# Four load buffers and an earlier queue place for the modulation in the first FFN rows, one power for the first norm

## The chip, the core and the metric

The kernel runs on one core of one Trainium2 chip. The metric is the device time of one execution in microseconds; lower is better. Three runs of the kernel before took 1579.51, 1582.39 and 1585.93 us, median 1582.39.

## The reference

One decoder block on x (256 tokens by 2048) with a condition vector c. Six modulation vectors of 2048 come from one large product with a single row, `mod = silu(c) @ w_ada + b_ada`, and w_ada is 2048 by 12288. The rest is matrix products with 256 rows:

```python
hn = rmsnorm(x, norm1_g) * (1 + sc1) + sh1
x = x + gt1 * hybrid_mixer(hn, ...)      # w_in, two causal mixers, dn_w_o, cf_w_o, w_out
hn = rmsnorm(x, norm2_g) * (1 + sc2) + sh2
gate, up = split(hn @ w_up)              # w_up 2048 x 11264
x = x + gt2 * ((silu(causal_dwconv(gate)) * up) @ w_down)
return rmsnorm(x, final_norm_g)
```

In the code the modulation pieces have the numbers j = 0 (sh1), 1 (sc1), 2 (gt1), 3 (sh2), 4 (sc2), 5 (gt2).

## The kernel before

**A product.** All large products go through `product` (L282). A weight comes in chunks of two rows of 128: a DMA of 512 KB into `w` (five buffers), ScalarE casts it to `wh` (L300, three buffers), VectorE takes the rest `wl = w - wh` (L302, three buffers), and TensorE does 12 matmuls of 512 columns with it (L289 to L291: two rows, two halves of the tokens, three terms). Two PSUM banks hold the result until `evac` takes it.

**The modulation runs beside the products.** `ada_block` (L131) makes one piece for one range of rows: for each of 16 rows of w_ada a load `ada_w` (L153, on SP's queue, 384 KB where the range is 768 wide), and a multiply-add of the loaded row on VectorE into `ada_acc` (L162). After the sixteenth row the sums over the partitions are taken: on TensorE six transposes of `ada_acc` (L86, tile `pt`), on VectorE a reduce of those (L191) and one addition that gives `mod` (L200). `ada_block` is a generator; `product` takes `side_rate` steps of it with each chunk (`credit`), and `need` (L211) takes all that is left of the named pieces at once.

**The FFN's first rows.** The 16 rows of w_up are cut into ranges, R3 = (0,4), (4,10), (10,16), so that products can start before all of hn2 is there. Of 22 products with w_up the first 12 (six groups, gate and up) run over range 0 (called part 0 here: 24 chunks, 288 matmuls), then all over range 1 (part 1: 36 chunks, 432 matmuls), then over range 2 together with what follows. Their sums stay in the tiles `part`. While part 0 runs, pieces 4 and 3 of the modulation are made for range 1, and while part 1 runs, for range 2. `modulate2(part)` (L889) then makes the range's tiles of hn2: `xn` (the norm's factor, L897 on ScalarE, L898 on VectorE), transposes (`turned`), and `split` (L257): `t` (L260, VectorE), hn's high part (L261, ScalarE), hn's low part (L262, VectorE). It needs `mod` of its range.

**What sets the order.** Each engine runs its own queue in order. The queues are made by a scheduler that plays the program through with bands of priority (`b_w`, `b_first`, `b_ada`), buffers and `issue_after` edges, so a change in one place can move instructions elsewhere too. A load waits on SP's queue until its buffer is free, and holds what stands behind it there.

**The first norm.** `rstd_col` (L223) gives the factor of one half of the tokens: a reduce on VectorE (L226), an addition (L227) and a power (L229) on GpSimd. L348 calls it for each half; then come eight scalings of `xt` (L352), transposes, and the sums of the first modulation pieces.

Later named in the text: the p1 stage (L396 on, 14 products over columns of w_in, each for two ranges, beside which pieces 1 and 0 of the modulation are made for the next range), and the cfo product (branch b's output, weights cf_w_o), which starts after a layer norm, whose silu pieces are `cfa` (L794) and whose input tiles are `cfh` (L828), beside the small matmuls of the DeltaNet (`bank`).

Of the kernel before, what the change touches and what calls it, by code (L numbers as in the profile page):

```python
# [55 lines left out]
def block_kernel(ctx: ExitStack, tc, x, vec, ab, rowv, w_ada, w_in, dn_w_o, cf_w_o, w_out, w_up, w_down, out):  # L56
# [28 lines left out]
    def turn(out, in_, n=P):  # L85
        nc.tensor.transpose(out=out, in_=in_, identity=ident[0:n, 0:n])  # L86
# [30 lines left out]
    A1, A2 = ([p0.tile([P, k1 - k0], F32, name=f"A{i}{k0}") for k0, k1 in R3] for i in (1, 2))  # L117
    av = w_ada.rearrange("(k p) n -> p k n", p=P)

    last_ada = [None]  # L120
    gt_rows, gt_home = {}, {}

    def gt_row(j, piece):
# [7 lines left out]
    def ada_block(j, part, pool, bufs, band=None, shared=False):  # L131
# [17 lines left out]
            pt = ps.tile([P, 512], F32, tag="tp", name="pt")  # L149
        for kc in range(0, KD, step):  # L150
            with band():
                wt = pool.tile([P, step, n], F32, tag="ada_w", bufs=bufs, name="ada_w")
                last_ada[0] = nc.sync.dma_start(out=wt, in_=av[:, kc:kc + step, c0:c0 + n]).ins  # L153
                for i in range(step):
                    k = kc + i
                    if shared and k % 3 == 2 and k < KD - 2:
                        for m in range(nk):
                            nc.tensor.matmul(pt[:, m:m + 1], lhsT=wt[:, i, m * P:(m + 1) * P], rhs=c_act[:, k:k + 1], start=(k == 2 and m == 0), stop=False, skip_group_check=True)
                    elif k == 0 and not as_row:
                        nc.vector.tensor_scalar(out=acc[:, 0:n], in0=wt[:, i, :], scalar1=c_act[:, k:k + 1], scalar2=None, op0=ALU.mult)  # L160
                    else:
                        nc.vector.scalar_tensor_tensor(out=acc[:, 0:n], in0=wt[:, i, :], scalar=c_act[:, k:k + 1], in1=acc[:, 0:n], op0=ALU.mult, op1=ALU.add)  # L162
            if kc + step < KD:
                yield
# [58 lines left out]
    def rstd_col(ms, t):  # L223

        a = p0.tile([P, 1], F32, tag="nrm_h", bufs=2, name="nrm_h")
        last_sum[0] = nc.vector.tensor_reduce(out=a, in_=ms[:, t, :], axis=mybir.AxisListType.X, op=ALU.add).ins  # L226
        nc.gpsimd.tensor_scalar(out=a, in0=a, scalar1=EPS, scalar2=None, op0=ALU.add)  # L227
        r = p0.tile([P, 1], F32, tag="nrm_c", bufs=2, name="nrm_c")
        nc.gpsimd.tensor_tensor(out=r, in0=a, in1=mhalf[:, 0:1], op=ALU.pow)  # L229
        return r  # L230
# [40 lines left out]
    def turned(src, tiles, pool=ps, tag="tp"):  # L271

        bank = pool.tile([P, 2, S], F32, tag=tag, name="turned")
        for i, j in enumerate(tiles):
            for t in range(2):
                turn(bank[:, i, t * P:(t + 1) * P], src[:, t, j * P:(j + 1) * P])
        return bank


# [43 lines left out]
    def rows(W, c0, k0=0):  # L323
        v = W.rearrange("(k p) n -> p k n", p=P)
        return lambda w, kc: [(w, v[:, k0 + kc:k0 + kc + 2, c0:c0 + 512])]
# [9 lines left out]
    with b_first():  # L335
        x_sb = p0.tile([P, KD, S], F32, tag="x", name="x_sb")
        xv = x.rearrange("(t p) n -> p t n", p=P)
        xt = p1.tile([P, 2, D], F32, tag="HS", name="xt")
        for q in range(2):
            for t in range(2):  # L340
                nc.sync.dma_start(out=xt[:, t, q * 1024:(q + 1) * 1024], in_=xv[:, t, q * 1024:(q + 1) * 1024])
        nc.sync.dma_start(out=vt, in_=vec)
        ss1 = p0.tile([P, 2, 2], F32, name="ss1")
        for q in range(2):
            for t in range(2):
                sq = p1.tile([P, 1024], F32, tag=("QA", "KA")[t], name="sq")
                nc.scalar.activation(out=sq, in_=xt[:, t, q * 1024:(q + 1) * 1024], func=AF.Square, scale=D ** -0.5, accum_out=ss1[:, t, q:q + 1])
        r1 = [rstd_col(ss1, t) for t in range(2)]  # L348
        for q in range(4):
            qs = slice(q * 512, (q + 1) * 512)  # L350
            for t in range(2):
                nc.vector.tensor_scalar(out=xt[:, t, qs], in0=xt[:, t, qs], scalar1=r1[t], scalar2=None, op0=ALU.mult)  # L352
            for i in range(2):
                k = 4 * q + 2 * i
                nc.scalar.copy(out=x_sb[:, k:k + 2, :], in_=turned(xt, (k, k + 1), pd, f"dl{i}"))
        for j in (1, 0):
            drain(ada_block(j, 0, sup, 6, shared=True))
        hn = p0.tile([P, 2, KD, S], F32R, tag="hn", name="hn")
        modulate(0)
# [529 lines left out]
    def modulate2(part):  # L889
        k0, k1 = R3[part]  # L890
        with b_first():
            xn = p2.tile([P, 2, (k1 - k0) * P], F32, tag="raw", name="xn")

            for a, b in ((k0, k0 + 2), (k0 + 2, k1)) if part == 0 else ((k0, k1),):
                at_ = slice((a - k0) * P, (b - k0) * P)
                with tc.issue_after(ada_after[0]) if part else nullcontext(), tc.issue_after(ada_after[1]) if part else nullcontext():
                    nc.scalar.activation(out=xn[:, 0, at_], in_=res[:, 0, a * P:b * P], func=AF.Copy, scale=r2[0])  # L897
                    nc.vector.tensor_scalar(out=xn[:, 1, at_], in0=res[:, 1, a * P:b * P], scalar1=r2[1], scalar2=None, op0=ALU.mult)  # L898
            for k in range(0, k1 - k0, 2):
                bank = turned(xn, (k, k + 1), pd, f"dl{k // 2 % 2}")  # L900
                for i in range(2):
                    c = slice(k + i, k + i + 1)
                    after = split(hn2, k0 + k + i, bank[:, i, :], A2[part][:, c], mod[3][part][:, c])
        return after
# [3 lines left out]
    ada_after[:] = modulate2(0)  # L908

    NG = 6  # L910
    pre = [p2.tile([P, 2, 512], F32, tag=f"h{g}{i}", name=f"part{g}{i}") for g in range(NG) for i in range(2)]
    for part in range(2):
        side_rate[0] = (1.2, 0.9)[part]
        for g in range(NG):
            for i, off in enumerate((0, FF)):
                product("up1", rows(w_up, off + 512 * g), R3[part], gh, gl, into(both(pre[2 * g + i]), part > 0))
        need((4, part + 1), (3, part + 1))
        modulate2(part + 1)
    for half, (g0, g1) in enumerate(((0, 6), (6, 11))):
        nt = 4 * (g1 - g0)  # L920
        hf = {}
# [38 lines left out]
            product("gate", rows(w_up, 512 * g), ks, gh, gl, evac_gate)  # L960
            product("up", rows(w_up, FF + 512 * g), ks, gh, gl, evac_up)
        if half == 0:
            raw = p2.tile([P, 2, D], F32, tag="raw", name="raw")
            for g in range(4):
                product("down", rows(w_down, 512 * g, 4 * g0), (0, nt), lambda k: hf[k // 4][0][:, k % 4, :], lambda k: hf[k // 4][1][:, k % 4, :], into(both(raw, g), False))
            continue
        need((5, 0), (5, 1))
        fg_row = p2.tile([P, D], F32, name="fg_row")
        nc.sync.dma_start(out=fg_row, in_=rowv[:, 2 * D:].to_broadcast([P, D]))
        with b_ada():  # L970
            for g in range(4):
                for d, r in zip(both(raw, g), both(res, g)):
                    nc.vector.tensor_tensor(out=d, in0=d, in1=gt_row(5, g), op=ALU.mult)
                    nc.vector.tensor_tensor(out=r, in0=d, in1=r, op=ALU.add)
        for g in range(4):
# [63 lines left out]
```

## Time and profile before

| | us |
|---|---|
| median of three runs | 1582.39 |
| profiled execution, device time | 1579.35 |
| profiled execution, span of the trace | 1577.6 |
| TensorE busy | 1522.2 (96%) |
| TensorE idle, the difference | 55.4 |
| VectorE busy | 1188.6 (75%) |
| ScalarE busy | 812.1 (51%) |
| GpSimd busy | 58.0 (4%) |

The profiled execution lies 3.0 us below the median. TensorE is busy all the time but for some 55 us, so the question for any change is which of those idle stretches it fills, and whether it opens new ones. The views that matter are the table of windows (busy time of each engine in a stretch, the granted clock PEclk, the busy share of the DMA engines and what they moved), and the timelines of the engines around an idle stretch, where a bracket says how long the engine stood idle before an instruction and which result ended the wait. Consecutive instructions overlap a little at their ends, so the step from one start to the next is shorter than the printed length.

### The profile page before, as it was taken

The page shows a single profiled execution, that of the slowest core. Times are in us where ns is not written, and L with a number is a line of the kernel's source. Part 1 is how long each engine was busy: PE and PEld are TensorE (multiplying, and loading weights), DVE is VectorE, ACT ScalarE, POOL GpSimd, SP SyncE. Part 2 cuts the span into 40 slices and gives each one's busy share as a digit, 9 for nine tenths or more (in the row PEclk, how much of TensorE's full clock was granted, in tenths as well). Part 3 has the DMA queues.
Part 4 walks back from the last instruction along what each step waited for, and adds up shares of the span by engine and source line. Part 5 has one row for each costly group of instructions (what it writes and reads, how often), then busy time and mean ns, then how long its engine had stood idle before and what let it go on. Part 6 is the DMA issues. An engine that isn't in the chain of part 4 may idle for free. (4 is left out here: it accounts for less than half of the span.)

```text
span 1577.6 us, 20092 instructions
## 1 busy us (share of the span) xinstructions
PE 1522.2 (96%) x7198; PEld 1257.7 (80%) x7198; DVE 1188.6 (75%) x1558; ACT 812.1 (51%) x1222; POOL 58.0 (4%) x120
## 2 busy tenths in 40 slices
PE   5999999999999999999989899999999999999997
PEld 5788887788888878788868687888888878888885
DVE  5889977689998978897577899887445677775554
ACT  3554444777687455544445334555434445454443
POOL 2000000400002000000000000000000000000000
PEclk9999999999999999999989999999999999999999
DMA  9999966534567738889779898655556777765552
GB/s 322 387 361 345 297 189 178 162 115 130 150 220 227 238 107 260 276 287 333 234 237 321 278 318 293 205 171 174 190 190 217 265 248 244 258 202 187 187 187 107
DMA packets 182284, 366.59 MB, mean 232 GB/s; under 512 B 12452, under 2 KB 30884, under 8 KB 182056
## 3 DMA queue, kind: packets, MB, share of 16 engines
q1 hardware_dynamic: 182184, 365.31, 69.6%
q8 instruction: 56, 0.92, 0.2%
q14 instruction: 44, 0.36, 0.1%
HBM read 363.17 MB, written 2.10 MB: 232 GB/s over the span
## 5 line engine op out<-in xcount | busy, mean ns | idle before, releaser
L300 ACT CAST wh<-w 128x1024 fp32r<-128x1024 f32 x488 | 512.8, 1052 | 579.4 <-PE mm_up L290 136.6
L302 DVE TENSOR_TENSOR wl<-w,wh 128x1024 fp32r<-128x1024 f32 x488 | 593.4, 1220 | 235.6 <-ACT wh L300 233.5
L162 DVE SCALAR_TENSOR_TENSOR ada_acc<-ada_w,c_act,ada_acc 128x768 f32<-128x768 f32 (+2 forms) x236 | 242.5, 1028 | 80.4 <-DMA ada_w<-in_w_ada 75.2
L290 PE MATMUL mm_up<-wh,hn 128*128 128x512 f32 x472 | 185.7, 394 | 2.9 <-DVE hn L262 2.9
L289 PE MATMUL mm_up<-wh,hn 128*128 128x512 f32 x472 | 184.8, 396 | 1.3 <-ACT wh L300 0.5
L291 PE MATMUL mm_up<-wl,hn 128*128 128x512 f32 x472 | 173.8, 396 | 1.5 <-DVE wl L302 1.4
L289 PE MATMUL mm_down<-wh,h 128*128 128x512 f32 x352 | 139.1, 395 | 0.0
L290 PE MATMUL mm_down<-wh,h 128*128 128x512 f32 x352 | 138.9, 395 | 0.0
L291 PE MATMUL mm_down<-wl,h 128*128 128x512 f32 x352 | 125.6, 395 | 0.0
L289 PE MATMUL mm_p<-wh,hn 128*128 128x512 f32 x280 | 109.4, 395 | 2.7 <-ACT hn L261 2.7
L290 PE MATMUL mm_p<-wh,hn 128*128 128x512 f32 x280 | 109.4, 392 | 0.0
L290 PEld LDWEIGHTS mm_up<-wh,hn 128*128 128x128 f32 x472 | 89.4, 190 | 21.6 <-DVE hn L262 3.4
L291 PEld LDWEIGHTS mm_up<-wl,hn 128*128 128x128 f32 x472 | 89.1, 189 | 21.7 <-DVE wl L302 3.5
L289 PEld LDWEIGHTS mm_up<-wh,hn 128*128 128x128 f32 x472 | 89.6, 190 | 20.4 <-issue 1.0
L291 PE MATMUL mm_p<-wl,hn 128*128 128x512 f32 x280 | 99.2, 392 | 0.0
L289 PE MATMUL mm_gate<-wh,hn 128*128 128x512 f32 x232 | 91.7, 395 | 0.0
L290 PE MATMUL mm_gate<-wh,hn 128*128 128x512 f32 x232 | 90.5, 390 | 0.0
L291 PE MATMUL mm_gate<-wl,hn 128*128 128x512 f32 x232 | 85.0, 392 | 0.2 <-DVE wl L302 0.2
L291 PEld LDWEIGHTS mm_down<-wl,h 128*128 128x128 f32 x352 | 66.3, 188 | 15.4
L290 PEld LDWEIGHTS mm_down<-wh,h 128*128 128x128 f32 x352 | 66.3, 188 | 15.4
L289 PEld LDWEIGHTS mm_down<-wh,h 128*128 128x128 f32 x352 | 66.3, 188 | 15.3
L441 DVE SCALAR_TENSOR_TENSOR cfa<-u,vt,cfa 128x256 f32<-128x256 f32 x176 | 75.8, 476 | 0.3
(308 smaller groups left out, 2483.3 us busy)
## 6 DMA issues: line engine op xcount, KB each, us to landing
w<-in_w_up SPq DMA_DIRECT2D x176, 512.0 KB, 4.4
w<-in_w_in SPq DMA_DIRECT2D x130, 512.0 KB, 4.2
ada_w<-in_w_ada SPq DMA_DIRECT2D x96, 512.0 KB, 4.9
ada_w<-in_w_ada SPq DMA_DIRECT2D x128, 384.0 KB, 5.3
w<-in_w_down SPq DMA_DIRECT2D x88, 512.0 KB, 3.6
w<-in_w_in SPq DMA_DIRECT2D x64, 256.0 KB, 3.9
w<-in_w_out SPq DMA_DIRECT2D x32, 512.0 KB, 5.5
w<-in_cf_w_o SPq DMA_DIRECT2D x16, 512.0 KB, 4.1
```

Of the source, the lines that this page charges most:

```text
L162: nc.vector.scalar_tensor_tensor(out=acc[:, 0:n], in0=wt[:, i, :], scalar=c_act[:, k:k + 1], in1=acc[:, 0:n], op0=ALU.mult, op1=ALU.add)
L289: nc.tensor.matmul(pts[t], lhsT=xh(k)[:, ts], rhs=wh, start=(k == k0), stop=False)
L290: nc.tensor.matmul(pts[t], lhsT=xl(k)[:, ts], rhs=wh, start=False, stop=False)
L291: nc.tensor.matmul(pts[t], lhsT=xh(k)[:, ts], rhs=wl, start=False, stop=(k == k1 - 1))
L300: nc.scalar.copy(out=wh, in_=w)
L302: nc.vector.tensor_tensor(out=wl, in0=w, in1=wh.bitcast(F32), op=ALU.subtract)
L441: nc.vector.scalar_tensor_tensor(out=acc[:, i, :], in0=us[g][:, i, k:k + S], scalar=V("cfconv", (2 * g + i) * CFK + k), in1=acc[:, i, :], ...
```

## The change

Three edits, of which two touch the FFN's first rows.

- **Load buffers.** In parts 0 and 1 every other load of `ada_w` goes to one of two further tiles (`raw2`, `raw3` in the pool `p2`), beside the two buffers it had. The tile `raw` of the later down product is cut into four tiles raw0 to raw3, and `xn` into two, raw0 and raw1.
- **Rate and place.** The rate of modulation steps is raised from 1.2 to 1.4 a chunk in part 0 and from 0.9 to 1.0 in part 1; `need` moves from behind the last product of a part to ahead of it; and the modulation steps that follow are ordered behind the newest range's row tiles (`ada_after` is set again for each part), where before they were ordered behind range 0's.
- **First norm.** One reduce, one addition and one power for both halves of the tokens.

```diff
@@ ada_block
-                wt = pool.tile([P, step, n], F32, tag="ada_w", bufs=bufs, name="ada_w")
+                if more[0] and kc // step % 2:
+                    wt = more[0].tile([P, step, n], F32, tag=f"raw{2 + kc // step // 2 % 2}", name="ada_w")
+                else:
+                    wt = pool.tile([P, step, n], F32, tag="ada_w", bufs=bufs, name="ada_w")
@@ first norm
-        r1 = [rstd_col(ss1, t) for t in range(2)]
+        a1 = p0.tile([P, 2], F32, name="a1")
+        nc.vector.tensor_reduce(out=a1, in_=ss1, axis=mybir.AxisListType.X, op=ALU.add)
+        nc.gpsimd.tensor_scalar(out=a1, in0=a1, scalar1=EPS, scalar2=None, op0=ALU.add)
+        nc.gpsimd.tensor_tensor(out=a1, in0=a1, in1=mhalf[:, 0:2], op=ALU.pow)
+        r1 = [a1[:, t:t + 1] for t in range(2)]
@@ modulate2
-            xn = p2.tile([P, 2, (k1 - k0) * P], F32, tag="raw", name="xn")
+            xn = [p2.tile([P, (k1 - k0) * P], F32, tag=f"raw{t}", name="xn") for t in range(2)]
@@ the FFN's first rows
+    more[0] = p2
     for part in range(2):
-        side_rate[0] = (1.2, 0.9)[part]
+        side_rate[0] = (1.4, 1.0)[part]
         for g in range(NG):
             for i, off in enumerate((0, FF)):
+                if (g, i) == (NG - 1, 1):
+                    need((4, part + 1), (3, part + 1))
+                    side_rate[0] = 0
                 product("up1", rows(w_up, off + 512 * g), R3[part], gh, gl, into(both(pre[2 * g + i]), part > 0))
-        need((4, part + 1), (3, part + 1))
-        modulate2(part + 1)
+        ada_after[:] = modulate2(part + 1)
@@ first down product
-            raw = p2.tile([P, 2, D], F32, tag="raw", name="raw")
+            more[0] = None
+            raw = [p2.tile([P, 2, 512], F32, tag=f"raw{g}", name="raw") for g in range(4)]
```

The scheduler's queues differ from before at several places. Line numbers of the changed kernel are three higher from L153 on, and seven to eleven higher behind L348.

**TensorE, part 0 of the FFN.** `pt<-ident,ada_acc` are the transposes with which the sums of piece 3 for range 1 begin. Before:

```order
L290 MATMUL mm_up_7634<-wh,hn_7041 128x512
L291 MATMUL mm_up_7634<-wl,hn_7041 128x512
L289 MATMUL mm_up_7635<-wh,hn_7041 128x512
L86 MATMUL pt<-ident,ada_acc 128x128 x6
L290 MATMUL mm_up_7635<-wh,hn_7041 128x512
L291 MATMUL mm_up_7635<-wl,hn_7041 128x512
L289 MATMUL mm_up_7634<-wh,hn_7041 128x512
```

These matmuls belong to the twelfth and last product of part 0; 274 of the part's 288 matmuls stand ahead of the transposes. Of the changed kernel:

```order
L293 MATMUL mm_up_7497<-wh,hn_7035 128x512
L294 MATMUL mm_up_7497<-wl,hn_7035 128x512
L292 MATMUL mm_up_7498<-wh,hn_7035 128x512
L86 MATMUL pt<-ident,ada_acc 128x128 x6
L293 MATMUL mm_up_7498<-wh,hn_7035 128x512
L294 MATMUL mm_up_7498<-wl,hn_7035 128x512
L292 MATMUL mm_up_7497<-wh,hn_7035 128x512
```

They now stand in the ninth product: 202 of the 288 matmuls are ahead of them. In part 1 the same transposes, for range 2, stood behind 634 of the 720 matmuls of both parts, and now stand behind 564; those of piece 4 move from 74 to 48, and from 436 to 384.

**SP, from the load of `fg_row` on, as part 0 begins.** Before:

```order
L969 DMA fg_row<-in_rowv 128x2048
L153 DMA ada_w<-in_w_ada 128x768 x3
L298 DMA w<-in_w_up 128x2x512
L153 DMA ada_w<-in_w_ada 128x768 x2
L298 DMA w<-in_w_up 128x2x512 x2
L153 DMA ada_w<-in_w_ada 128x768
L298 DMA w<-in_w_up 128x2x512 x3
L153 DMA ada_w<-in_w_ada 128x768 x2
L298 DMA w<-in_w_up 128x2x512
L153 DMA ada_w<-in_w_ada 128x768
L298 DMA w<-in_w_up 128x2x512
L153 DMA ada_w<-in_w_ada 128x768
```

Of the changed kernel:

```order
L980 DMA fg_row<-in_rowv 128x2048
L156 DMA ada_w<-in_w_ada 128x768 x6
L301 DMA w<-in_w_up 128x2x512
L156 DMA ada_w<-in_w_ada 128x768 x2
L301 DMA w<-in_w_up 128x2x512 x2
L156 DMA ada_w<-in_w_ada 128x768
L301 DMA w<-in_w_up 128x2x512
L156 DMA ada_w<-in_w_ada 128x768
L301 DMA w<-in_w_up 128x2x512
L156 DMA ada_w<-in_w_ada 128x768 x2
L301 DMA w<-in_w_up 128x2x512
L156 DMA ada_w<-in_w_ada 128x768
```

Eight loads of w_up stand ahead of this place in both. Behind it six modulation loads now stand in a row, where three stood. Counted on, of 18 loads left for the sums at the end of part 0 the last stands behind 11 further loads of w_up (18 before), and of 50 for those of part 1 the last stands behind 40 (48 before).

**ScalarE, from the activation table for silu to the last input of the cfo product's first rows.** Before:

```order
L613 COPY T_4128<-bank 64x256
L794 ACT_TABLE_LOAD
L794 ACTIVATE cfa_2983<-cfa_2983,vt 128x256 x2
L600 COPY P_3872<-bank 64x4x64
L794 ACTIVATE cfa_3133<-cfa_3133,vt 128x256 x2
L794 ACTIVATE cfa_3283<-cfa_3283,vt 128x256 x2
L828 CAST cfh<-cfa_2983 128x512
L600 COPY P_3920<-bank 64x4x64
L794 ACTIVATE cfa_3433<-cfa_3433,vt 128x256 x2
```

Of the changed kernel:

```order
L801 ACT_TABLE_LOAD
L801 ACTIVATE cfa_2977<-cfa_2977,vt 128x256 x2
L801 ACTIVATE cfa_3127<-cfa_3127,vt 128x256 x2
L835 CAST cfh<-cfa_2977 128x512
L801 ACTIVATE cfa_3277<-cfa_3277,vt 128x256 x2
L613 COPY U_3909<-bank 32x4x32 x2
L620 COPY T_4100<-bank 64x256
```

The first `cfh` now stands behind four silu pieces, where it stood behind six and a copy of `P`. On TensorE the first cfo matmuls now stand ahead of eight small matmuls of the DeltaNet that they stood behind.

## Rows read from the trace of the kernel before

**Rows 1.** The page, busy time of each engine and one of the costliest groups.

```profile
PE 1522.2 (96%) x7198; PEld 1257.7 (80%) x7198; DVE 1188.6 (75%) x1558; ACT 812.1 (51%) x1222; POOL 58.0 (4%) x120
...
L162 DVE SCALAR_TENSOR_TENSOR ada_acc<-ada_w,c_act,ada_acc 128x768 f32<-128x768 f32 (+2 forms) x236 | 242.5, 1028 | 80.4 <-DMA ada_w<-in_w_ada 75.2
```

**Rows 2.** Six windows of 20 us; columns are named in the first line.

```profile
core 0: us, PE busy (x) PEld busy (x) DVE busy (x) ACT busy (x) POOL busy (x), PEclk, DMA share, GB/s
580.00:600.00 20.00, 16.87 (x114) 12.83 (x113) 11.93 (x17) 14.35 (x34) 1.68 (x2) 0.83 0.29 84
840.00:860.00 20.00, 20.00 (x90) 16.57 (x89) 14.85 (x15) 11.95 (x16) 0.00 (x0) 1.00 0.94 327
860.00:880.00 20.00, 14.76 (x64) 11.37 (x63) 16.29 (x23) 8.95 (x14) 0.00 (x0) 0.91 0.89 302
880.00:900.00 20.00, 19.68 (x89) 15.98 (x88) 17.71 (x24) 7.52 (x9) 0.00 (x0) 1.00 0.80 256
940.00:960.00 20.00, 19.37 (x86) 15.20 (x85) 17.40 (x20) 7.38 (x7) 0.95 (x1) 1.00 0.91 308
960.00:980.00 20.00, 19.17 (x85) 15.19 (x84) 19.26 (x28) 8.41 (x12) 0.00 (x0) 1.00 0.84 282
```

**Rows 3.** Timeline of PE, 864 to 880 us: start, length, engine, line, operation, wait before.

```profile
864.21 0.81 PE L86 MATMUL pt<-ident,ada_acc 128*128 128x128 f32 x6
...
870.07 0.66 PE L86 MATMUL turned<-ident,xn 128*128 128x128 f32 x4 [1.81 <-DVE t L260]
...
874.11 0.80 PE L290 MATMUL mm_up<-wh,hn 128*128 128x512 f32 x1 [2.92 <-DVE hn L262]
...
877.62 0.40 PE L290 MATMUL mm_up<-wh,hn 128*128 128x512 f32 x1
...
879.19 0.50 PE L289 MATMUL mm_up<-wh,hn 128*128 128x512 f32 x1 [0.50 <-ACT wh L300]
```

**Rows 4.** Timeline of DVE, 801 to 874 us.

```profile
801.63 2.06 DVE L162 SCALAR_TENSOR_TENSOR ada_acc<-ada_w,c_act,ada_acc 128x768 f32<-128x768 f32 x2
...
862.22 1.02 DVE L162 SCALAR_TENSOR_TENSOR ada_acc<-ada_w,c_act,ada_acc 128x768 f32<-128x768 f32 x1 [0.66 <-DMA ada_w<-in_w_ada]
...
865.43 1.01 DVE L191 TENSOR_REDUCE ada_t<-pt 128x4 f32<-128x512 f32 x2
...
871.57 1.02 DVE L162 SCALAR_TENSOR_TENSOR ada_acc<-ada_w,c_act,ada_acc 128x768 f32<-128x768 f32 x1 [1.56 <-DMA ada_w<-in_w_ada]
872.50 1.22 DVE L302 TENSOR_TENSOR wl<-w,wh 128x1024 fp32r<-128x1024 f32 x1
873.64 0.75 DVE L262 TENSOR_TENSOR hn<-t,hn 128x256 fp32r<-128x256 f32 x2
```

**Rows 5.** Groups by line, DVE, 801.0 to 865.3 us: count, busy, mean ns, idle before.

```profile
L302 DVE TENSOR_TENSOR wl<-w,wh 128x1024 fp32r<-128x1024 f32 x22 | 26.6, 1218 | 0.4 <-ACT wh L300 0.4
L162 DVE SCALAR_TENSOR_TENSOR ada_acc<-ada_w,c_act,ada_acc 128x768 f32<-128x768 f32 x21 | 21.4, 1018 | 13.9 <-DMA ada_w<-in_w_ada 13.5
```

**Rows 6.** Timeline of PE, sums of the third range.

```profile
957.85 0.81 PE L86 MATMUL pt<-ident,ada_acc 128*128 128x128 f32 x6
```

**Rows 7.** Timeline of PE, first matmuls of the cfo product.

```profile
592.49 1.22 PE L289 MATMUL mm_cfo<-wh,cfh 128*128 128x512 f32 x2 [1.93 <-ACT cfh L828]
```

**Rows 8.** Timeline of POOL, first norm.

```profile
11.08 0.57 POOL L229 TENSOR_TENSOR nrm_c<-nrm_h,mhalf 128x1 f32<-128x1 f32 x1
...
13.51 0.74 POOL L229 TENSOR_TENSOR nrm_c<-nrm_h,mhalf 128x1 f32<-128x1 f32 x1
```

**Rows 9.** Timeline of DVE, third and fourth sums of the p1 stage.

```profile
150.45 1.01 DVE L162 SCALAR_TENSOR_TENSOR ada_acc<-ada_w,c_act,ada_acc 128x768 f32<-128x768 f32 x1
...
156.72 0.17 DVE L200 TENSOR_TENSOR mod<-pt,vt 128x6 f32<-128x6 f32 x1 [2.40 <-PE pt L180]
...
191.09 1.01 DVE L162 SCALAR_TENSOR_TENSOR ada_acc<-ada_w,c_act,ada_acc 128x768 f32<-128x768 f32 x1
...
198.82 0.15 DVE L200 TENSOR_TENSOR mod<-pt,vt 128x6 f32<-128x6 f32 x1
```

More of the change, by code (lines that the diff above doesn't have):

```diff
@@ L118, in block_kernel @@
     av = w_ada.rearrange("(k p) n -> p k n", p=P)
-    last_ada = [None]
+    last_ada, more = [None], [None]
     gt_rows, gt_home = {}, {}
@@ L275, in turned @@
             for t in range(2):
-                turn(bank[:, i, t * P:(t + 1) * P], src[:, t, j * P:(j + 1) * P])
+                turn(bank[:, i, t * P:(t + 1) * P], (src[t] if isinstance(src, list) else src[:, t, :])[:, j * P:(j + 1) * P])
         return bank
@@ L896, in modulate2 @@
                 with tc.issue_after(ada_after[0]) if part else nullcontext(), tc.issue_after(ada_after[1]) if part else nullcontext():
-                    nc.scalar.activation(out=xn[:, 0, at_], in_=res[:, 0, a * P:b * P], func=AF.Copy, scale=r2[0])
-                    nc.vector.tensor_scalar(out=xn[:, 1, at_], in0=res[:, 1, a * P:b * P], scalar1=r2[1], scalar2=None, op0=ALU.mult)
+                    nc.scalar.activation(out=xn[0][:, at_], in_=res[:, 0, a * P:b * P], func=AF.Copy, scale=r2[0])
+                    nc.vector.tensor_scalar(out=xn[1][:, at_], in0=res[:, 1, a * P:b * P], scalar1=r2[1], scalar2=None, op0=ALU.mult)
             for k in range(0, k1 - k0, 2):
@@ L962, in block_kernel @@
         if half == 0:
-            raw = p2.tile([P, 2, D], F32, tag="raw", name="raw")
+            more[0] = None
+            raw = [p2.tile([P, 2, 512], F32, tag=f"raw{g}", name="raw") for g in range(4)]
             for g in range(4):
-                product("down", rows(w_down, 512 * g, 4 * g0), (0, nt), lambda k: hf[k // 4][0][:, k % 4, :], lambda k: hf[k // 4][1][:, k % 4, :], into(both(raw, g), False))
+                product("down", rows(w_down, 512 * g, 4 * g0), (0, nt), lambda k: hf[k // 4][0][:, k % 4, :], lambda k: hf[k // 4][1][:, k % 4, :], into(both(raw[g]), False))
             continue
@@ L971, in block_kernel @@
             for g in range(4):
-                for d, r in zip(both(raw, g), both(res, g)):
+                for d, r in zip(both(raw[g]), both(res, g)):
                     nc.vector.tensor_tensor(out=d, in0=d, in1=gt_row(5, g), op=ALU.mult)
```

## The prediction

> **What bounds the kernel now.** I read the page's busy times first, then the windows over the span, then the timelines of the engines around each window in which TensorE is not busy for all of its time. The page shows a TensorE that works 1522.2 us of a span of 1577.6 [rows 1]: a change can win only in the 55 us of idle time, and in what the slower clock costs after them. The windows show where these lie: of those that the change can reach, 5.24 us at 860 to 880, 0.32 at 880 to 900, 0.63 and 0.83 at 940 to 980, and 3.13 at 580 to 600 (20 less PE's busy time [rows 2]). The start has some more.
>
> The stall at 864 to 880 is a chain. TensorE's transposes for the sums of piece 3 start at 864.21, with only 14 matmuls of the part behind them [rows 3]; VectorE reduces them at 865.43 [rows 4], and the row tiles of the next range need the result. TensorE waits 1.81 us for `t` and 2.92 us for hn's low part [rows 3]. The second wait is VectorE's queue: hn's low part starts at 873.64, behind a modulation step that itself sat 1.56 us waiting for its load, and behind a `wl` [rows 4]. The eight matmuls from 874.11 until 877.62 take 3.51 us [rows 3], where 90 in 20 us [rows 2] would take eight 1.78: the granted clock of the window is .91 [rows 2], and the matmuls behind the pause run at the lower of the two levels, 1.2 GHz in place of 2.4.
>
> Why the sums are so late: VectorE waits for loads of w_ada. From 801.0 to 865.3 it sits idle for 13.5 us for these loads, beside 21.4 us of steps and 26.6 us of `wl` [rows 5]; over the kernel the wait is 75.2 us [rows 1].
>
> **The change part by part.** All sums are against the profiled execution, 1579.35 us, which is 3.0 us under the median of the runs.
>
> *End of part 0.* The transposes of the sums move from behind 274 matmuls to behind 202, 72 x 0.222 = 16.0 us earlier, to about 848.2. The row tiles then have some 19 us (86 matmuls) before part 1's first product wants them; in the trace of before the way from the transposes to hn's low part took 873.64 - 864.21 = 9.4 us, with a load's wait in it. So the whole stall goes: idle 5.24 + 0.32, and 3.51 - 1.78 = 1.73 us of slow clock, 7.3 us. I leave 0.6 for the wait for a cast that stands in it too (0.50 at 879.19 [rows 3]): **-6.7**. What must hold for it is that the loads come sooner. Ahead of the sums stand, from VectorE's step at 801.63 on [rows 4], 18 loads of 0.393 MB and 11 of 0.524, 12.8 MB; until 848.2 less 1.5 us for the last steps that asks for 286 GB/s. The windows with two buffers moved 327 GB/s at a share of .94, 302 at .89, 256 at .80 and 308 at .91 [rows 2]; divided by the share, 320 to 348 GB/s with the DMA engines full, which four buffers bring nearer. VectorE's own work in that time, 21 steps of 1.02 and 14 `wl` of 1.22 by their means [rows 5], is 39 us of the 45.
>
> *End of part 1.* The same transposes stood at 957.85 [rows 6]; 70 matmuls earlier, less the 7.3 us won before, is 935. The idle 0.63 + 0.83 goes but for a little: **-1.3**. Here it is tight. 50 loads of w_ada and 40 of w_up, 40.6 MB, by 933.5 from 801.6 ask for 308 GB/s, and the lowest full rate above, 320, has them there at 928.5. VectorE's steps between the two sums (30 steps, 28 `wl`, 14 additions to `part`, the row tiles) come to 82 us by the printed means, and 77 by the steps from start to start, which are some 0.08 shorter (872.50 to 873.64 for a `wl` of 1.22 [rows 4]); there are 87. Between a stall of nothing and one of some 8 us, at 290 GB/s, I take nothing, since the rate that I ask for lies under all the full rates.
>
> *Layer norm and cfo.* A side effect of the scheduler. TensorE waited 1.93 us for `cfh` at 592.49 [rows 7], the window has 3.13 us of idle time and a clock of .83 [rows 2]. `cfh` now stands behind four silu pieces instead of six and a copy, and some small DeltaNet matmuls that ran before it now follow. At most the 3.13 us and a part of the clock go, some 4 us; at the least nothing, if the copies that moved behind are then waited for. I take the middle: **-2.0**.
>
> *First norm.* Of two powers, at 11.08 (0.57) and 13.51 (0.74) [rows 8], one stays, but it must wait for all four squares, so the first scalings come later and the last one at about the same time, half a us late. VectorE's first row tile stands ahead of one `wl` more, which is a step of 1.14 us [rows 4]. Between -1.1 and +0.7 I take **-0.4**, as the row tile is what the first product waits for.
>
> *p1 stage.* Here the queue moves the third and fourth sums 28 and 59 matmuls, 6.2 and 13.1 us, ahead. TensorE never waited there. After the last step (ends 151.46) `mod` came 5.3 us later, and after that of the fourth (ends 192.10) 6.7 us later [rows 9]; TensorE's sums take about 1.4 of these, so the slack was 3.9 and 5.3. If VectorE were no earlier, TensorE would now stall for 2.3 + 7.8 = 10 us; but ahead of the third sums its queue now holds two `wl` fewer, and ahead of the fourth seven and two additions, 2.3 and some 9 us of work: with the slack that covers 6.2 and 13.1, and the lower end is nothing. I take **+1.0**, near that end. The last sums, of piece 5, also move ahead, by 48 and 148 matmuls, where loads come singly; I put 0, and up to 2 in the range.
>
> The remaining waits (out product to FFN at 780 to 800, the end) keep their order: 0. **Sum:** -6.7 - 1.3 - 2.0 - 0.4 + 1.0 = -9.4, so 1570.0 on the profiled execution's scale, and with its 3.0 us to the median 1573.0, 0.6% faster. About 0.5%, 7.9 us, is what a measurement of this kernel can tell from no change.
>
> **The rivals.** *A, the loads hold TensorE at the earlier sums.* SP's queue is in order: a load of w_ada that waits for its buffer holds back the weights behind it, and the change puts more of them ahead of the weights. Up to the end of part 1 the lead of the weights over TensorE falls from 56 chunks issued at chunk 53 to 48 at chunk 47. For it: with two buffers some windows moved only 256 and 282 GB/s [rows 2], and VectorE was busy for 17.7 and 19.3 us of 20 in them. Against: the share was .80 and .84 in just these, so the DMA engines lacked loads, not speed. At 288 GB/s the 40.6 MB are there 9.4 us late, and all that is won is lost; at 270, within those rows, the stall is 18.4 us, with the slow clock behind it (1.7) the kernel takes 1579.35 - 9.4 + 20.1 = 1590.1, on the median's scale 1593. From 275 GB/s down it is slower by more than that 0.5%. The Trainium skill (DMA: Bandwidth & Descriptors, Anatomy of one DMA) says that DMA engines don't wait on semaphores: any wait happens on the issuing sequencer before dispatch. By that rule a blocked modulation load does hold the weights, and the trace of before agrees in so far as the share sank to .80 while VectorE waited for loads.
>
> *B, the p1 stage and the layer norm give it back.* The stall in the FFN goes, but TensorE waits at the earlier p1 sums, nearer the upper end (+6), and the layer norm's place wins nothing: 1579.35 - 6.7 - 1.3 - 0.4 + 6 = 1577, on the median's scale 1580, within 0.5%. For it: the slack of 3.9 and 5.3 us [rows 9] is less than the move. Against: VectorE's queue moved by the difference.
>
> *C, the change doesn't do what it says.* The two added buffers fill no sooner, since loads wait on SP behind weights that wait for theirs; the sums come when they came, and TensorE waits at them instead of at the row tiles. Of -8.0 at the two ends perhaps 3 is left: 1579.35 - 3 - 2 - 0.4 + 1 = 1575, on the median's scale 1578, within 0.5%.
>
> **How the numbers follow.** My forecast 0.60, A 0.14 (0.09 of it slower by over 0.5%), B 0.12, C 0.14. Of the forecast's own case 0.08 ends within 0.5%, by the spread of the layer norm and p1 terms; that gives faster 0.52, same 0.08 + 0.05 + 0.12 + 0.14 = 0.39, slower 0.09. Its own range is 1564 to 1579: the lower end takes -4 at the layer norm, -1.1 at the start, 0 in p1 and -7.3 at part 0's end, with the runs' 3 us under the median; the upper end takes 0 and +5 there. The range that holds 8 in 10 reaches on to B and C and to A's milder half: 1564 to 1585.
>
> **What would show it.** Right: no idle TensorE above 1 us between 840 and 980 and PEclk 1.00 there, the transposes of the sums at about 848 and 935 (some us earlier by what was won ahead), VectorE's wait for w_ada from 801 to 865 well under 13.5 us, and a DMA share near 1 at over 320 GB/s. The cfo product would start some 3 us earlier. Wrong: TensorE waiting for `ada_acc` at the transposes or for `wl` behind them (A); waits for `ada_acc` at the p1 sums (B); a wait for w_ada as long as before (C).

## The result and the profile after

Four runs of the changed kernel took 1562.68 to 1567.94 us, median 1564.44, against 1581.77 for four of the kernel before: ratio 0.9886, interval 0.9872 to 0.9900. It is 17.3 us faster, where 9.4 were forecast. A second set of six runs, later (e11 below), gave 1565.38 and ratio 0.9892 (0.9874 to 0.9910). The profiled execution took 1565.42 us, with a span of 1563.7.

The page after has less idle time of TensorE than the table before ([rows 1] and span: 55.4 us; now 51.4), but also 9.9 us less busy time for the same 7198 matmuls, which no part of the prediction had:

```profile
PE 1512.3 (97%) x7198; PEld 1252.9 (80%) x7198; DVE 1187.4 (76%) x1557; ACT 809.5 (52%) x1222; POOL 55.3 (4%) x118
...
L165 DVE SCALAR_TENSOR_TENSOR ada_acc<-ada_w,c_act,ada_acc 128x768 f32<-128x768 f32 (+2 forms) x236 | 242.3, 1027 | 51.3 <-DMA ada_w<-in_w_ada 49.8
```

The windows, with the columns of [rows 2] and one more stretch, 700 to 720:

```profile
core 0: us, PE busy (x) PEld busy (x) DVE busy (x) ACT busy (x) POOL busy (x), PEclk, DMA share, GB/s
580.00:600.00 20.00, 18.19 (x100) 12.78 (x98) 13.23 (x16) 14.35 (x29) 0.95 (x1) 0.91 0.44 129
700.00:720.00 20.00, 15.58 (x68) 11.94 (x67) 15.69 (x20) 6.28 (x7) 0.00 (x0) 1.00 0.96 352
840.00:860.00 20.00, 20.00 (x93) 16.62 (x92) 17.51 (x22) 11.21 (x15) 0.00 (x0) 1.00 0.99 358
860.00:880.00 20.00, 20.00 (x96) 16.54 (x95) 19.10 (x25) 12.51 (x18) 0.00 (x0) 1.00 0.91 317
880.00:900.00 20.00, 20.00 (x93) 16.62 (x92) 18.22 (x24) 7.38 (x7) 0.00 (x0) 1.00 0.96 342
940.00:960.00 20.00, 20.00 (x92) 16.55 (x91) 20.00 (x28) 9.98 (x14) 0.00 (x0) 1.00 0.77 248
960.00:980.00 20.00, 20.00 (x90) 16.57 (x89) 18.70 (x19) 7.72 (x8) 0.00 (x0) 1.00 0.84 283
```

In the FFN's first rows the forecast holds. From 840 to 980 TensorE is busy for all of the time and PEclk is 1.00, where 860 to 880 had 14.76 and .91. The DMA engines move 358 GB/s at a share of .99 in 840 to 860, where two buffers brought 327 at .94. The timeline of PE shows no wait at the sums and at the row tiles (compare [rows 3] and [rows 6]):

```profile
851.51 0.82 PE L86 MATMUL pt<-ident,ada_acc 128*128 128x128 f32 x6
...
861.26 0.60 PE L86 MATMUL turned<-ident,xn 128*128 128x128 f32 x4
...
873.09 0.38 PE L86 MATMUL turned<-ident,xn 128*128 128x128 f32 x2
...
876.08 0.81 PE L86 MATMUL turned<-ident,xn 128*128 128x128 f32 x6
...
936.37 0.82 PE L86 MATMUL pt<-ident,ada_acc 128*128 128x128 f32 x6
```

The transposes of the sums run at 851.51, those of the next range at 936.37, and the part's end is not waited for. The FFN now begins 4.0 us later (first mm_up at 802.49, before 798.51), so 851.51 is 49.0 us after its begin; the forecast 848.2 was 49.7. VectorE's wait for w_ada in the same window as [rows 5] falls from 13.5 to 1.6 us, with 26 steps in it where there were 21:

```profile
L165 DVE SCALAR_TENSOR_TENSOR ada_acc<-ada_w,c_act,ada_acc 128x768 f32<-128x768 f32 x26 | 26.3, 1013 | 1.9 <-DMA ada_w<-in_w_ada 1.6
L305 DVE TENSOR_TENSOR wl<-w,wh 128x1024 fp32r<-128x1024 f32 x20 | 24.4, 1222 | 3.1 <-ACT wh L303 3.0
```

The window 700 to 720 tells the other way: 15.58 us busy, where the kernel before had 19.92:

```profile
700.00:720.00 20.00, 19.92 (x94) 16.32 (x93) 17.07 (x22) 9.32 (x15) 0.00 (x0) 1.00 0.93 336
```

TensorE waits for weights in the out product: five waits with 5.98 us of idle time from its first matmul to its last, where the kernel before had one of 0.08. These are rows of PE, ScalarE and VectorE of the changed kernel there:

```profile
717.49 0.50 PE L292 MATMUL mm_out<-wh,mg 128*128 128x512 f32 x1 [2.28 <-ACT wh L303]
...
719.68 0.74 PE L294 MATMUL mm_out<-wl,mg 128*128 128x512 f32 x2 [0.98 <-DVE wl L305]
```

```profile
716.39 1.04 ACT L303 CAST wh<-w 128x1024 fp32r<-128x1024 f32 x1 [3.03 <-DMA w<-in_w_out]
```

```profile
717.74 0.75 DVE L165 SCALAR_TENSOR_TENSOR ada_acc<-ada_w,c_act,ada_acc 128x512 f32<-128x512 f32 x1 [3.01 <-DMA ada_w<-in_w_ada]
```

ScalarE waited 3.03 us for a load of w_out, VectorE 3.01 us for a load of w_ada, while the DMA engines were nearly full (share .96 in that window). The queue suggests why: loads of the modulation and of x stand ahead of the weight. On SP's queue of the changed kernel, two loads of w_ada and four of x (512 KB each) stand with one weight between them just ahead of that place; before, the modulation loads stood singly there, and a weight stood among the loads of x.

The place of the whole difference, by the first and last matmul of each product (column before to after, both profiled executions, us):

| stretch | before | after | difference |
|---|---|---|---|
| start to first mm_p | 42.98 | 40.91 | -2.07 |
| p1 stage (to first mm_qkv) | 198.52 | 200.05 | +1.53 |
| to last mm_ga | 331.87 | 329.11 | -2.76 |
| last mm_ga to first mm_cfo | 19.12 | 15.64 | -3.48 |
| first mm_cfo to first mm_out | 106.29 | 109.16 | +2.87 |
| first to last mm_out | 91.02 | 98.92 | +7.90 |
| to first mm_up | 8.71 | 8.70 | 0 |
| first mm_up to first mm_gate (FFN's first rows) | 179.42 | 168.59 | -10.83 |
| to first mm_down | 110.66 | 110.16 | -0.50 |
| first to last mm_down | 477.02 | 470.42 | -6.60 |

Two of the large differences, +7.9 and -6.6, lie where I had put 0. The third row, -2.76, has no cause in the change: kernels with the same queues there give 329.0 to 331.9 from one execution to the next.

### The profile page after: what moved, and what is told of

It is laid out like the page before. It is cut to its first block, busy times and chain, and to the rows that moved or that the text cites. A ratio compares the mean times of both kernels' runs of the same rounds, so it can differ in the third digit from the quotient of the medians.

```text
span 1563.7 us, 20087 instructions
## 1 busy us (share of the span) xinstructions
PE 1512.3 (97%) x7198; PEld 1252.9 (80%) x7198; DVE 1187.4 (76%) x1557; ACT 809.5 (52%) x1222; POOL 55.3 (4%) x118
## 5 line engine op out<-in xcount | busy, mean ns | idle before, releaser
L294 PE MATMUL mm_up<-wl,hn 128*128 128x512 f32 x472 | 170.5, 393 | 0.0
L292 PE MATMUL mm_down<-wh,h 128*128 128x512 f32 x352 | 137.2, 390 | 0.0
L293 PE MATMUL mm_down<-wh,h 128*128 128x512 f32 x352 | 136.9, 389 | 0.0
L293 PEld LDWEIGHTS mm_down<-wh,h 128*128 128x128 f32 x352 | 66.1, 188 | 13.7
L294 PEld LDWEIGHTS mm_down<-wl,h 128*128 128x128 f32 x352 | 66.1, 188 | 13.7
L292 PEld LDWEIGHTS mm_down<-wh,h 128*128 128x128 f32 x352 | 66.1, 188 | 13.5
```

What stands on the lines that cost most here:

```text
L292: nc.tensor.matmul(pts[t], lhsT=xh(k)[:, ts], rhs=wh, start=(k == k0), stop=False)
L293: nc.tensor.matmul(pts[t], lhsT=xl(k)[:, ts], rhs=wh, start=False, stop=False)
L294: nc.tensor.matmul(pts[t], lhsT=xh(k)[:, ts], rhs=wl, start=False, stop=(k == k1 - 1))
```

## The experiments

The experiments are numbered e1 to e12; each is named where it begins.

**The slower matmuls of the down product.** The mean step from the start of one matmul to the next, by the timeline and without the steps across waits and at the lower clock, was 0.2324 us in mm_down, 0.2324 in mm_cfo and 0.2329 in mm_dno before, and 0.2265, 0.2289 and 0.2276 after, at PEclk 1.00 in both; mm_up, mm_gate and mm_p had 0.227 to 0.228 in both. For mm_down the page's groups show the same as the mean length of one. Before:

```profile
L289 PE MATMUL mm_down<-wh,h 128*128 128x512 f32 x352 | 139.1, 395 | 0.0
L290 PE MATMUL mm_down<-wh,h 128*128 128x512 f32 x352 | 138.9, 395 | 0.0
```

After:

```profile
L292 PE MATMUL mm_down<-wh,h 128*128 128x512 f32 x352 | 137.2, 390 | 0.0
L293 PE MATMUL mm_down<-wh,h 128*128 128x512 f32 x352 | 136.9, 389 | 0.0
```

No instruction of these products differs. What differs is where tiles lie: in the built program every tile from p0's later part on lies elsewhere. The first theory, and its test (e1), an unused tile at the place of `a1`:

```diff
+        p0.tile([P, 2], F32, name="pad")
         r1 = [rstd_col(ss1, t) for t in range(2)]
```

> The kernel before with one unused tile of 8 bytes a partition in p0 at the place where the change puts a1: no instruction moves, but every later tile of SBUF lies 32 bytes higher. Theory 'offset' (matmuls whose stationary tiles lie behind p0 ran at a step of 0.2324 us before and 0.2265 after because those tiles moved by 32 bytes): step of mm_down 0.227, of mm_cfo and mm_dno too, 1056 x 0.0059 + 384 x 0.005 = about 8 us less than before, ratio 0.995. Rival 'other' (the split of raw, the queues' order, or the run set the step): step 0.232 and ratio 1.000.

Measured: ratio 1.0006 (0.9988 to 1.0023), steps 0.2330 in mm_down and 0.2330 in mm_dno.

```profile
L289 PE MATMUL mm_down<-wh,h 128*128 128x512 f32 x352 | 139.4, 396 | 0.0
L290 PE MATMUL mm_down<-wh,h 128*128 128x512 f32 x352 | 138.8, 394 | 0.0
```

The theory falls: moving every later tile by 32 bytes does nothing. The converse (e2), the changed kernel with such a tile behind `a1`:

```diff
         a1 = p0.tile([P, 2], F32, name="a1")
+        p0.tile([P, 2], F32, name="pad")
```

> The changed kernel with the same unused tile added, so that its tiles lie 32 bytes past a multiple of 64 again; no instruction moves. 'Offset': step of mm_down 0.232, about 8 us slower than the change, near 1572. 'Other': as the change, 1564.

Measured: 1565.17 us, ratio to before 0.9894 (0.9877 to 0.9910), step of mm_down 0.2271. The theory falls here too. But of the four kernels that ran together the two with the first norm's edit (e2 and e4, below) had the short step and the two without it (e1 and e3) the long one: the edit does set it, by something else than 32 bytes. In the built programs the tiles of the first norm have other places in p0 after the edit, which moves hn, w, wh and wl by 96 bytes down and the tiles of the pools behind p0 by 32 up. The address of a product's stationary tile less that of the first `wh`, modulo 256:

| stationary tile, product | before | after | e1 | e2 |
|---|---|---|---|---|
| hn, mg: mm_p, mm_up, mm_gate, mm_out | 0 | 0 | 0 | 0 |
| cfh, DeltaNet's output, h: mm_cfo, mm_dno, mm_down | 128 | 0 | 128 | 0 |

The address of h alone, modulo 256, can't be it: it is 64 both in the change (step 0.2265) and in e1 (0.2330).

The second theory, a distance, with a tile that moves the pools behind p0 alone (e5):

```diff
+    p0.tile([P, 32], F32, name="pad")
     r2, r3 = [], []
```

> The kernel before with an unused tile of 128 bytes a partition at the end of p0: hn, w, wh and wl stay, the tiles of the pools behind p0 (cfh, the DeltaNet's output, h) lie 128 bytes higher, and no instruction moves. Theory 'distance' (the step of a matmul is 0.232 us where its stationary tile lies 128 bytes past a multiple of 256 from wh, and 0.227 at a multiple of 256; before 128 for cfo, dno and down, 0 for all products over hn and mg; the change 0 for all): step of mm_down 0.2265, mm_dno 0.2275; 1056 x 0.0059 + 384 x 0.005 = 8 us less than before, ratio 0.995. Rival 'queue' (the order that the first norm's edit sets off makes the step): 0.232, ratio 1.000.

Measured: ratio 0.9964 (0.9948 to 0.9979), 6.3 us less by the medians; steps 0.2271 in mm_down, 0.2274 in mm_dno, 0.2287 in mm_cfo. The groups:

```profile
L289 PE MATMUL mm_down<-wh,h 128*128 128x512 f32 x352 | 137.2, 390 | 0.0
L290 PE MATMUL mm_down<-wh,h 128*128 128x512 f32 x352 | 137.0, 389 | 0.0
```

The same line in the changed kernel, at the same place (e6):

```diff
+    p0.tile([P, 32], F32, name="pad")
     r2, r3 = [], []
```

> The changed kernel with the same unused tile of 128 bytes at the end of p0, which puts the stationary tiles of cfo, dno and down 128 bytes past a multiple of 256 from wh. 'Distance': step of mm_down 0.232, 8 us slower than the change, near 1572 to 1573. 'Queue': 0.2265, 1564 to 1565.

Measured: 1572.77 us (1567.9 to 1575.18), 7 to 8 us over the change; step of mm_down 0.2330, of mm_dno 0.2325. The groups:

```profile
L292 PE MATMUL mm_down<-wh,h 128*128 128x512 f32 x352 | 139.7, 397 | 0.0
L293 PE MATMUL mm_down<-wh,h 128*128 128x512 f32 x352 | 138.6, 394 | 0.0
```

Adding and taking away agree, with no instruction moved: where these tiles lie relative to those of p0 sets the step. That it is the distance to `wh`, the tile that these matmuls read beside them, is the likeliest reading; `hn`, `w` and `wl` keep their places relative to `wh` in all these kernels. A third distance, 64 bytes more than before, so 192 (e10):

```diff
+    p0.tile([P, 16], F32, name="pad")
     r2, r3 = [], []
```

> The kernel before with an unused tile of 64 bytes a partition at the end of p0, no instruction moved: the stationary tiles of cfo, dno and down lie 192 bytes past a multiple of 256 from wh. If only a multiple of 256 is fast: step of mm_down 0.232, ratio 1.000. If only 128 is slow: 0.2265, ratio 0.996.

Measured: ratio 0.9976 (0.9963 to 0.9989), step of mm_down 0.2291. The groups:

```profile
L289 PE MATMUL mm_down<-wh,h 128*128 128x512 f32 x352 | 138.7, 394 | 0.0
L290 PE MATMUL mm_down<-wh,h 128*128 128x512 f32 x352 | 137.2, 390 | 0.0
```

Neither expectation: 192 lies between. Here only the group of L289 is long (394), the other is at 390.

**The parts of the change.** The FFN edits without the first norm's, with the tile of e1, so at distance 128 (e3); against the changed kernel:

```diff
-        a1 = p0.tile([P, 2], F32, name="a1")
...
-        r1 = [a1[:, t:t + 1] for t in range(2)]
+        p0.tile([P, 2], F32, name="pad")
+        r1 = [rstd_col(ss1, t) for t in range(2)]
```

> The FFN edits alone (buffers, rates, place of the sums) on the kernel before, with the unused tile, first norm as before. Up to the FFN its queues are those of before. Theory: 'offset' gives 8, the FFN's stretch 10.8 as in the change, and no TensorE waits for wl or wh in the out product appear, since those come from the order that the first norm's edit sets off: about 1563. Rival (the waits in the out product come with the FFN edits, whose loads move ahead): 1571, with waits of some 6 us for wl and wh at 700 to 760.

Measured: 1568.02 us, ratio 0.9914 (0.9896 to 0.9932); from the first mm_up to the first mm_gate 168.44 us; out product 91.1 us. The FFN's gain and the out product's loss are apart, as the theory had it; the 8 us of the first theory's placement are not there, so the time is higher by some 5 than the 1563 expected.

The first norm's edit alone (e4); against the kernel before:

```diff
-        r1 = [rstd_col(ss1, t) for t in range(2)]
+        a1 = p0.tile([P, 2], F32, name="a1")
+        nc.vector.tensor_reduce(out=a1, in_=ss1, axis=mybir.AxisListType.X, op=ALU.add)
...
+        r1 = [a1[:, t:t + 1] for t in range(2)]
```

> The first norm's edit alone; its new tile a1 also moves the later tiles by 32 bytes. Theory: start and layer norm win some 6, p1 loses 1.5 and the out product 8, as in the change, so the FFN begins 4 us later than before; the FFN's own stall stays; the down products win 6.2: about 2 us under before, ratio 0.9985. Rival (the out product's loss belongs to the FFN edits): 10 under before, ratio 0.994. If 'offset' is wrong: 4 us slower than before.

Measured: 1580.85 us, ratio 0.9997 (0.9983 to 1.0010). The out product takes 97.4 us, with these waits of TensorE from 690 to 770 (total, times, longest):

```profile
PE mm_out L291 <- DVE wl L302: 3.5, 4, 1.5
PE mm_out L289 <- ACT wh L300: 1.4, 1, 1.4
```

So the edit that was to save a power at the start wins 2 us there and some at the layer norm, gains 6 to 8 us by the distance, which it changes as a by-product, loses 2 in p1 and 6 to 7 in the out product by the order that it sets off, and ends where it began.

Only the FFN edits, at distance 0 (e7); against the changed kernel:

```diff
-        a1 = p0.tile([P, 2], F32, name="a1")
...
-        r1 = [a1[:, t:t + 1] for t in range(2)]
+        r1 = [rstd_col(ss1, t) for t in range(2)]
...
+    p0.tile([P, 32], F32, name="pad")
     r2, r3 = [], []
```

> The FFN edits alone, first norm as before, with the tile of 128 bytes at the end of p0. 'Distance': 8 us under the FFN edits with the other placement (1568.0), so 1560, and under the change, since the waits in the out product that the first norm's edit brings are not there. 'Queue': 1568.

Measured: 1562.04 us, ratio 0.9868 (0.9849 to 0.9886), 6.0 under e3 where 8 were expected. TensorE's only wait in the out product:

```profile
PE mm_out L292 <- ACT wh L303: 1.6, 1, 1.6
```

The buffers alone, with raw and xn cut as in the change (e8; the lines of that cut are left out here); against the kernel before:

```diff
+                if more[0] and kc // step % 2:
+                    wt = more[0].tile([P, step, n], F32, tag=f"raw{2 + kc // step // 2 % 2}", name="ada_w")
+                else:
...
+    more[0] = p2
...
+            more[0] = None
```

> The two further load buffers alone (raw and xn cut as in the change), with the rates, need and the order of before; first norm as before. In the queue the sums move as in the change in part 0 (behind 202 matmuls) and to 586 in part 1. Theory (the loads were what made the sums late, so the buffers carry the gain): from the first mm_up to the first mm_gate 169 to 171 us, as with all FFN edits (168.5; before 179.4); total about 1569 to 1571. Rival (the rates and the place of need carry it): 176 us or more, 1578 or more.

Measured: 1569.03 us, ratio 0.9904 (0.9880 to 0.9927); first mm_up to first mm_gate 169.20. Its windows, columns as above:

```profile
840.00:860.00 20.00, 20.00 (x95) 16.60 (x94) 17.59 (x23) 12.18 (x18) 0.00 (x0) 1.00 0.99 357
860.00:880.00 20.00, 20.00 (x94) 16.45 (x93) 18.93 (x24) 11.56 (x17) 0.00 (x0) 1.00 0.92 318
880.00:900.00 20.00, 20.00 (x93) 16.62 (x92) 18.23 (x24) 7.47 (x8) 0.00 (x0) 1.00 0.92 320
```

VectorE's wait for w_ada from 801.0 to 865.3:

```profile
L165 DVE SCALAR_TENSOR_TENSOR ada_acc<-ada_w,c_act,ada_acc 128x768 f32<-128x768 f32 x26 | 26.3, 1013 | 2.0 <-DMA ada_w<-in_w_ada 1.8
```

That is e3's time (1568.02) to within the noise, at the same distance: the buffers carry the gain. They do two things at once: the loads come sooner, and the scheduler puts the sums of part 0 behind 202 matmuls, where they stood behind 274. Which of the two would do alone was not tried. The rates and places alone (e9):

```diff
-        side_rate[0] = (1.2, 0.9)[part]
+        side_rate[0] = (1.4, 1.0)[part]
...
+                if (g, i) == (NG - 1, 1):
+                    need((4, part + 1), (3, part + 1))
+                    side_rate[0] = 0
...
-        need((4, part + 1), (3, part + 1))
-        modulate2(part + 1)
+        ada_after[:] = modulate2(part + 1)
```

> The raised rates, the earlier need and the order edges alone, with two load buffers and the first norm as before. In the queue the sums stay where they were (behind 274 matmuls in part 0, 649 in part 1). Theory (the loads are the limit): the stall at the end of part 0 stays, from the first mm_up to the first mm_gate 177 to 185 us, total as before, ratio 0.998 to 1.003. Rival (rates and place give part of the gain of 11): 174 us or less, ratio 0.996 or less.

Measured: ratio 0.9994 (0.9983 to 1.0005), stretch 180.94 us. The stall stays, with waits of 2.63 and 3.45 us, where the kernel before had 1.81 and 2.92:

```profile
861.98 0.82 PE L86 MATMUL pt<-ident,ada_acc 128*128 128x128 f32 x6
...
868.62 0.66 PE L86 MATMUL turned<-ident,xn 128*128 128x128 f32 x4 [2.63 <-DVE t L260]
...
873.18 0.80 PE L290 MATMUL mm_up<-wh,hn 128*128 128x512 f32 x1 [3.45 <-DVE hn L262]
```

VectorE's wait for w_ada in the same window stays too:

```profile
L162 DVE SCALAR_TENSOR_TENSOR ada_acc<-ada_w,c_act,ada_acc 128x768 f32<-128x768 f32 x20 | 20.4, 1018 | 15.4 <-DMA ada_w<-in_w_ada 15.1
```

Last, the change (e11) and the best version, that of e7 (e12), again, on one chip:

> The changed kernel again, beside the next kernel on one chip, to compare the two. As before: ratio 0.988 to 0.990.

> The FFN edits with the first norm as before and the tile of 128 bytes at the end of p0, again. If leaving the first norm's edit out wins what its order costs in the out product: some 2 to 3 us under the changed kernel on the same chip, ratio 0.986 to 0.988. If the lead of the earlier run came from the chip: the same as the change.

Measured: 1565.38 us (ratio 0.9892, 0.9874 to 0.9910) and 1563.38 (0.9874, 0.9853 to 0.9894). The best version lies 2.0 us under the change here and 2.4 in the earlier runs, which were on different chips; the intervals overlap, so that it is ahead is likely and not settled.

## Why the prediction was right or wrong

The direction was right and the size was wrong: 9.4 us were forecast, little more than half of the 17.3 measured, and the time lies only just inside the range. Two steps failed. The sum put at 0 whatever was not idle time of TensorE: the down products gained 6.6 us there and the out product lost 7.3. And it mis-sized the term that was right in kind, the stall at the ends of parts 0 and 1: 8.0 forecast, 10.8 in the profiled pair and 12.6 by the means.

That it lies inside is in part luck. Two terms that the sum had at 0, +7.90 in the out product and -6.60 in the down products, nearly cancel. And the lower end, 1564, is lower than its own terms: -4, -1.1, 0 and -7.3, with the -1.3 of part 1, give 1579.35 - 13.7 = 1565.7, which is above the measured 1564.44.

**End of parts 0 and 1: right in kind, too small.** Forecast -6.7 and -1.3; the stretch lost 10.83 us in the profiled pair, and 12.6 by the means below. The chain (loads, sums, row tiles) was right: e8 with buffers alone takes the stall away, e9 without them leaves it. Loads at 358 GB/s and VectorE's wait of 1.6 us are what the text asked for. Two steps mis-sized it. The first took the idle time of a wait for its price. The seven waits of the stretch have 6.71 us of idle time, but the steps across them are 7.74 us longer than the 0.227 of the others, since the idle time counts from the end of the printed length of a matmul (0.39), 0.16 past the start that the next one would have had. The lower clock cost 3.6 us in the stretch, and 1.6 of it are left after; the text had 1.73 to win. And the 0.6 left for the cast's wait went too. The second step was to price the stall from one profiled execution and to add the 3.0 us to the median unchanged. With two buffers the stretch took 179.4, 181.1, 182.5, 184.7, 180.9 and 179.6 us in six kernels' profiled executions (mean 181.4), with four 168.0 to 169.3 in eight (mean 168.8): the profile shown was the mildest case, and the gain is 12.6 us. The part of "3.0 us under the median" that comes from this stall goes with it.

**Rates and places: nothing of their own.** I priced them with the buffers and never apart. e9 shows that alone they do nothing that can be measured; beside the buffers they have at most 0.8 us of the stretch (169.20 in e8, 168.44 in e3).

**What was put at 0 without a reason.** This is the step that failed in kind: "a change can win only in the 55 us of idle time, and in what the slower clock costs after them", and "The remaining waits (out product to FFN at 780 to 800, the end) keep their order: 0". The profiled pair has 4.0 us less idle time and 9.9 us less busy time. The sum took the duration of a matmul as a constant of the kernel. The down products' 1056 matmuls went from 0.2324 to 0.2265; their steps sum to 245.5 us before and to 239.6 after (239.6 in e2, e4 and e5 too), 5.9 us of the 6.60 in the table, whose stretch also holds 960 matmuls of mm_gate and mm_up. cfo and dno go with them for 1 to 2. Nothing in the diff or the queues says so; the addresses in the built programs do, and the trace of before held a hint that I passed over: mm_down's step of 0.232 beside mm_up's 0.227, at one clock. The page's mean lengths hide it, with 395 ns for mm_down and 394 to 396 for mm_up.

**Out product: a loss that I had not seen.** I compared queues where TensorE was idle before, and put 0 for the rest. The out product had no idle time to look at, so I did not read its new order of loads; it costs 7 us (91.0 to 93.4 us in nine executions with the first norm as before, mean 91.7; 97.4 to 99.9 in five with the edit, mean 99.0). The steps across the five waits have 6.8 of the 7.9 us in the profiled pair. That two loads in a row and four of x hold the weights is read from the rows above; a kernel with this order undone and the norm's edit kept was not tried.

**First norm.** Forecast -0.4 at the start, measured -2.07; over all executions the first mm_p comes at 40.5 in the mean with the edit and 42.2 without. The scalings were read rightly: the last of them ends at 16.20, before at 15.95. That the row tile (`t`) stands ahead of one `wl` more was in the sum too. What was mis-sized is the end of the sums between them, which the text let come as late as the scalings. VectorE's last step for them ends at 36.95, before at 38.39, as it waits less for loads of w_ada behind the scalings (3.2 us, before 4.7). The row tile starts 2.56 us sooner. Before:

```profile
35.28 3.11 DVE L162 SCALAR_TENSOR_TENSOR ada_acc<-ada_w,c_act,ada_acc 128x512 f32<-128x512 f32 x4 [1.94 <-DMA ada_w<-in_w_ada]
...
41.91 0.73 DVE L260 TENSOR_SCALAR t<-x_sb,A,mod 128x256 f32<-128x256 f32 x2
```

After:

```profile
35.41 1.54 DVE L165 SCALAR_TENSOR_TENSOR ada_acc<-ada_w,c_act,ada_acc 128x512 f32<-128x512 f32 x2 [0.27 <-DMA ada_w<-in_w_ada]
...
39.35 0.73 DVE L263 TENSOR_SCALAR t<-x_sb,A,mod 128x256 f32<-128x256 f32 x2
```

**Layer norm.** Forecast -2.0, measured -3.48 from the last mm_ga to the first mm_cfo, whose own wait stays (compare [rows 7]):

```profile
585.71 0.73 PE L292 MATMUL mm_cfo<-wh,cfh 128*128 128x512 f32 x2 [1.81 <-ACT cfh L835]
```

From the last mm_ga to the first mm_dno, which holds the work that moved behind, the profiled pair wins nothing (77.12 before, 78.05 after). Over all executions the means are 79.8 without the first norm's edit (77.1 to 83.4) and 76.9 with it (74.8 to 78.7), so some 3; of these the distance has about 1, an estimate from the steps of mm_cfo. The size was right; what the moved `cfh` wins by itself was not tried apart.

**p1.** Forecast +1.0, measured +1.53 in the profiled execution and 2.1 by the means (198.1 and 200.2). The path is another, so that the number is near is luck: TensorE waits at no sum there, but twice for a `wl`. These two waits stand in all five executions with the first norm's edit and in none of the nine without it, and the steps across them have 1.2 us:

```profile
132.16 0.73 PE L294 MATMUL mm_p<-wl,hn 128*128 128x512 f32 x2 [0.72 <-DVE wl L305]
...
174.93 0.73 PE L294 MATMUL mm_p<-wl,hn 128*128 128x512 f32 x2 [0.16 <-DVE wl L305]
```

**The rivals.** A did not come: TensorE has no wait for weights or sums in parts 0 and 1, and the seven windows from 800 to 940 have 263 to 378 GB/s, 339 in the mean, where 308 was asked for. The Trainium skill's rule behind it (DMA: Bandwidth & Descriptors, Anatomy of one DMA, a section on DMAs issued from GpSimd, while these go from SP) is that a wait is taken on the issuing sequencer. The trace agrees: from 795 to 940 SP's queue stands 43.7 us, in 49 waits, until a step of VectorE frees a buffer of `ada_w`. But the weights behind these waits still came in time. B was right that something is given back, but not at the sums: p1 took 2, the out product 7. C fell with e8 and e9: VectorE's wait for loads is 1.8 us with the buffers alone and 15.1 without them.

In sum, with the means: start -1.7, p1 +2.1, layer norm to dno -2.9, out +7.3, FFN's first rows -12.6, down -6.6 (477.0 in the profile of before to 470.4), other stretches -1: -15.4, beside the measured -17.3 and -16.4; 1 to 2 us stay without a place.

## What to carry to other kernels

Where a small edit adds or removes a tile, compare the addresses of both builds before pricing anything by "the same instructions": here that alone was worth 6 to 8 us, about as much as the first norm's edit lost by its order. A stall that hangs on loads varies from run to run; take its price from several profiles, not from the mildest, and from the steps across the waits, not from their idle time. And read a scheduler's new queue also where TensorE was never idle, since that is where a loss can begin.

## What the runs showed of the hardware

The step of a matmul of 512 columns depended on where its stationary tile lay relative to the tiles of p0 in SBUF. By the distance to `wh` it was 0.2265 to 0.2271 us at a multiple of 256 bytes, 0.2291 at 192 past one, 0.2323 to 0.2330 at 128 past one, in mm_down at PEclk 1.00. Moving all of these tiles together by 32 bytes changed nothing, and the stationary tile's address alone did not set it. Products whose stationary tile was at distance 0 in every kernel (mm_up) stayed at 0.227. Why is open. Whether it is the distance to `wh`, to `wl` or to a tile that another engine uses was not taken apart: `wl` lies 12288 bytes past `wh`, so its distances are the same modulo 256.

Idle time understates a wait of TensorE: the seven waits in the FFN's first rows of the kernel before had 6.71 us of idle time and made the stretch 7.74 us longer.
